# The prompt scores of a differential attention: one fp32 product replaced by two fp32r products over stacked high and low parts

## The chip, the cores and the metric

The kernel runs on one core of a Trainium2 chip. The metric is the device time of one execution in microseconds (us). A profile is one execution taken apart by the hardware profiler; its engines are TensorE (PE, with PEld for its weight loads), VectorE (DVE), ScalarE (ACT), GpSimd (POOL) and SyncE (SP), which here only issues transfers.

## The reference, cut to what matters

One layer of a streaming encoder for 512 prompt tokens and 64 sample tokens, model width 1024, all in float32. A normed input goes through one input projection; its columns feed a gated-delta recurrence (GDN, 4 heads) and a differential attention (4 heads, two components c of 64 columns each for queries and keys, values of 128). Then follow an output projection, an attention over a memory, and a feed-forward stage. The attention that the change is about:

```
s = einsum('bqhcd,bkhcd->bhcqk', qi, kf) * 64 ** -0.5
visible = k_pos[None, :] < ((pi // CHUNK + 1) * CHUNK)[:, None]
s = where(visible, s, -inf)
p = softmax(s, axis=-1)
a = p[:, :, 0] - lam * p[:, :, 1]
return einsum('bhqk,bkhe->bqhe', a, vf)
```

The prompt attends to its own 512 keys in chunks of 64 (causal by chunk); the 64 sample tokens attend to 256 cached keys and their own 64.

## The kernel before, in words

Everything lies transposed, channels in the 128 partitions and tokens in the columns; prompt and sample tokens share one row of T = 576 columns. A weight matrix is loaded in blocks of 128 output columns. `weights` (L165) loads a block, casts it on ACT to its high part in fp32r (`wh`, L161) and subtracts on DVE (`wl`, L162). `project` (L169) multiplies such a block with the high and low parts of the input, in two halves of the tokens: columns 0 to 255 and 256 to 575 (n = 256 and 320). In the first half one multiplication of 512 columns does high weights times both parts of the input, and its two results come out side by side in a bank, to be added by `add_to` (L193: an ACT copy, L194, then a DVE addition, L195); the half has 16 multiplications. The second half has 24 of 320 columns and a single result. The results lie in one of three PSUM banks with the tag `pr`, until a function `evac` has read them.

The program is written in the order of the layer, but the framework orders the instructions of each engine itself: it takes what is ready by its own estimate of the times, earlier code first, and gives each tile a buffer of its tag. On the chip each engine then works through its list in that order, waiting on semaphores. A tile of a tag with one buffer can be written only when the one before has been read for the last time. Work of a later stage is thus found in the gaps of an earlier one. `tc.issue_after` puts instructions behind another one of the same engine.

The stages around the change, in the order of the code:

- GDN. `gdn_prep` (L651) prepares a chunk of 128 tokens for all four heads. Its triangular solve (L734 to L757) goes through levels of two matmul steps, a transpose, and ACT copies (L738 into `Y`, L742 into `X`), the last one L747 to L756, which reads `At` and `Dt`. There are four prompt chunks and a sample chunk; chunks of even number use the tags `At0`, `Dt0`, `Y0`, odd ones `At1`, `Dt1`, `Y1`, with one buffer each (L94). The tags `X`, `KQ` and `vb` have two buffers each for all chunks. `gdn_scan` (L782) then carries the state from chunk to chunk; `gdn_scan_sample` (L817) does the sample's, in pieces between the attention heads. The norms in them take a `pow` on POOL (`rpow`, L207, instruction on L208).
- `diff_project(h)` (L907) projects a head's queries, keys and values. Queries go from PSUM into `qz[h % 2]` (L912 to L919), a tile of two components, where component c has its 64 rows and zeros in the other 64; keys into `kdT` (L920 to L924), which holds all heads; values over a tile `zr` and a transpose into `vtm`. Keys are also transposed into `ko` (L936, which shares the two buffers of `p0`) and stored by SP (L938 to L941).
- `diff_cache` (L947) loads the cached keys and values; its first tile also has the tag `p0` (L948, loads on L951).
- `diff_head(h)` (L957) goes through five query tiles of 128, the sample's first (`t = 4`), then the prompt's four with 128, 256, 384 and 512 keys. For each component a score product goes into bank `g0` or `g1` (L975: the zero rows of `qz` take the other component's keys out of the sum, so `kdT`'s 128 rows serve both); then a maximum (L980), an exponential on ACT (L983), the combination of the two (L987, L988), a zeroing of the padding on POOL for `t = 4` (L990), transposes, and the product with the values. The head's norm, `finish` (L1006), runs in the next head (`between`, L965), with its `pow` on POOL.

The recurrence and the head loop (L1019 to L1026) are followed by the memory's keys and values, the output projection, the memory attention, whose queries are already split into high and low parts (L1160, L1161), and the feed-forward stage.

Of the kernel before, what the change touches and what calls it, by code (L numbers as in the profile page):

```python
# [8 lines left out]
F32 = mybir.dt.float32  # L9
F32R = mybir.dt.float32r  # L10
AF = mybir.ActivationFunctionType
ALU = mybir.AluOpType
# [3 lines left out]
P = 128  # L16
D = 1024
KT = 8
SEQ = 512
DEC = 64  # L20
T = SEQ + DEC
HALVES = ((0, 256), (256, T - 256))
PAST = 256
# [14 lines left out]
def hybrid_layer_kernel(  # L38
# [9 lines left out]
    nc = tc.nc  # L48
    V, A, G = nc.vector, nc.scalar, nc.gpsimd
# [17 lines left out]
    cp = ctx.enter_context(tc.tile_pool(name="cp", bufs=1))  # L67
# [24 lines left out]
    def small(tag, shape, bufs=None, dt=F32):  # L92
        tag = SHARED.get(tag, tag)
        bufs = 1 if tag in ("vn", "on", "S") or tag[:-1] in ("At", "Dt", "Y") else 2  # L94
        return sp.tile(shape, dt, tag=tag, name=nm(tag), bufs=bufs)
# [4 lines left out]
    def bank(tag="ba"):  # L100
        return ps.tile([P, 512], F32, tag=tag, name=nm(tag), bufs=BANKS[tag])
# [4 lines left out]
    def mm(out, lhsT, rhs, start=True, stop=True, pin=False, skip_group_check=False):  # L106
        i = nc.tensor.matmul(out, lhsT, rhs, start=start, stop=stop, skip_group_check=skip_group_check)  # L107
        if pin:
            tc.keep_in_program_order(i)
# [83 lines left out]
    def add_to(dst, b, more):  # L193
        A.copy(dst, more)  # L194
        V.tensor_tensor(dst, b, dst, ALU.add)  # L195
# [244 lines left out]
    for typ in (1, 0, 2):  # L440
# [3 lines left out]
        for h in range(H):  # L444
# [8 lines left out]
            n = SOFF + DEC  # L453
# [21 lines left out]
    with tc.issue_after(behind_keys[1]):  # L475
        ones2, triu2 = const([P, P], "ones2"), const([P, P], "triu2")
        G.memset(ones2, 0.0)
        for i in range(2):
            R = slice(i * DEC, (i + 1) * DEC)
            G.memset(ones2[R, R], 1.0)  # L480
        G.tensor_tensor(triu2, triu, ones2, ALU.mult)
# [8 lines left out]
    V.memset(wab2.bitcast(F32)[:, :, 16:], 0.0)  # L490
    A.copy(wab2[:, :, :8], wab)
    V.tensor_tensor(wab2[:, :, 8:16], wab, wab2.bitcast(F32)[:, :, :8], ALU.subtract)
    abT = small("p0", [16, T + DEC])
    for a0, n in HALVES:
        b = bank("pr")
        for k in range(KT):
# [6 lines left out]
    b = bank()  # L503
# [17 lines left out]
    t1, t2, t3 = gt("t1"), gt("t2"), gt("t3")  # L521
# [19 lines left out]
    def halves_of(dst, src):  # L541

        for i in range(2):
            R = slice(i * DEC, (i + 1) * DEC)
            V.tensor_copy(dst[R], src[R, 4, i::2])

# [24 lines left out]
    for j in range(3):  # L571
        b = bank()
# [321 lines left out]
    od, kdT = e3[:, 0], e5[:, 0]  # L894
# [2 lines left out]
    cv2 = view(e3, 1, 4, 4 * P).rearrange("p (i b) n -> p i b n", i=2)  # L897
    ckT, cvv = cv2[:, 0].rearrange("p b (c n) -> p (b c) n", n=PAST), cv2[:, 1]

    qz = [cp.tile([P, 2, T], F32, tag=f"qz{i}", name=f"qz{i}") for i in range(2)]  # L900
    with tc.issue_after(behind_keys[0]), tc.issue_after(behind_keys[1]):
        for q2 in qz:
            G.memset(q2[64:, 0, :], 0.0)
            G.memset(q2[:64, 1, :], 0.0)
        G.memset(vs[64:], 0.0)

    def diff_project(h):  # L907
        hs = slice(h * P, (h + 1) * P)
        for kind, base in (("q", 2056), ("k", 2568), ("v", 3080)):
            def evac(b, a0, n, more):  # L910
                ts_ = slice(a0, a0 + n)
                if kind == "q":  # L912
                    for c in range(2):
                        R = slice(64 * c, 64 * c + 64)
                        if more is not None:
                            add_to(qz[h % 2][R, c, ts_], b[R], more[R])
                        else:
                            (A.copy if c else V.tensor_copy)(qz[h % 2][R, c, ts_], b[R])
                    return  # L919
                d = small("zr", [P, 320])[:, :n] if kind == "v" else kdT[:, h, ts_]  # L920
                if more is not None:
                    add_to(d, b, more)
                else:
                    V.tensor_copy(d, b)  # L924
                bt = bank()
                for t in range(2):
                    tr(bt[:, t * P : (t + 1) * P], d[:, t * P : (t + 1) * P])
                if a0:
                    tr(bt[:DEC, 256:384], d[:, 256:])
                src, t2 = bt[:, :256].rearrange("p (t d) -> p t d", t=2), slice(a0 // P, a0 // P + 2)  # L930
                if kind == "v":
                    A.copy(vtm[:, t2, hs], src)
                    if a0:
                        A.copy(vs[:DEC, h, :], bt[:DEC, 256:384])
                else:
                    ko = small("ko", [P, 3, P])  # L936
                    A.copy(ko[:, :2], src)
                    nc.sync.dma_start(o_dk_p[0, 0, a0 : a0 + 256, h, :].rearrange("(t p) d -> p t d", p=P), ko[:, :2])  # L938
                    if a0:
                        A.copy(ko[:DEC, 2], bt[:DEC, 256:384])  # L940
                        nc.sync.dma_start(o_dk_s[0, 0, :, h, :], ko[:DEC, 2])  # L941

            project(weights(w2, base + h * P), xs, evac)
        nc.sync.dma_start(o_dv_p[0, 0, :, h, :].rearrange("(t p) d -> p t d", p=P), vtm[:, :, hs])
        nc.sync.dma_start(o_dv_s[0, 0, :, h, :], vs[:DEC, h, :])
# [11 lines left out]
    def diff_head(h, between):  # L957


        hs = slice(h * P, (h + 1) * P)  # L960
        so, co = tiny([P, 5], "ta"), tiny([P, 5], "ta")
        on = small("an", [P, 5, P])
        for t in (4, 0, 1, 2, 3):
            if t == 1:
                between()  # L965
            q0 = QT[t][0]
            nk = q0 + P if t < 4 else PAST + DEC
            nb = (nk + P - 1) // P
            pr = []
            mx, l = tiny([P, 2], "ta"), tiny([P, 2], "ta")  # L970
            for c in range(2):
                b = bank(f"g{c}")
                qq = qz[h % 2][:, c, q0 : q0 + P]
                if t < 4:
                    mm(b[:, :nk], qq, kdT[:, h, :nk])  # L975
                    V.memset(b[:64, nk - 64 : nk], -1e30)
                else:
                    mm(b[:, :PAST], qq, ckT[:, h, :])
                    mm(b[:, PAST:nk], qq, kdT[:, h, SEQ:T])
                V.tensor_reduce(mx[:, c : c + 1], b[:, :nk], AX.X, ALU.max)  # L980
                V.tensor_scalar(mx[:, c : c + 1], mx[:, c : c + 1], -0.125, None, ALU.mult)
                p = small(f"p{c}", [P, 512])
                A.activation(p[:, :nk], b[:, :nk], AF.Exp, bias=mx[:, c : c + 1], scale=0.125, accum_out=l[:, c : c + 1])  # L983
                pr.append(p)
            V.reciprocal(l, l)
            V.tensor_tensor(l[:, 1:2], l[:, 1:2], nlam, ALU.mult)
            V.tensor_scalar(pr[1][:, :nk], pr[1][:, :nk], l[:, 1:2], None, ALU.mult)  # L987
            V.scalar_tensor_tensor(pr[0][:, :nk], pr[0][:, :nk], l[:, 0:1], pr[1][:, :nk], ALU.mult, ALU.add)  # L988
            if nk < nb * P:
                G.memset(pr[0][:, nk : nb * P], 0.0)  # L990
            bt = bank()
            aT = small("aT", [P, 4, P])
            for kb in range(nb):
                tr(bt[:, kb * P : (kb + 1) * P], pr[0][:, kb * P : (kb + 1) * P])
            A.copy(aT[:, :nb, :], v4(bt, nb))
            po = bank("gs")[:, :P]
            for kb in range(nb):
                if t < 4:
                    vv = vtm[:, kb, hs]
                else:  # L1000
                    vv = cvv[:, kb, hs] if kb < 2 else vs[:, h, :]
                mm(po, aT[:, kb, :], vv, start=kb == 0, stop=kb == nb - 1)
            A.activation(pr[1][:, :P], po, AF.Square, accum_out=so[:, t : t + 1])
            A.copy(on[:, t, :], po)

        def finish():  # L1006
            V.tensor_scalar(so, so, 1.0 / P, EPS, ALU.mult, ALU.add)
            rpow(co, so)
            V.tensor_tensor(on, on, co.unsqueeze(2).to_broadcast([P, 5, P]), ALU.mult)
            b, b2 = bank(), bank()  # L1010
            for t in range(4):
                tr(b[:, t * P : (t + 1) * P], on[:, t, :])
            tr(b2[:, :P], on[:, 4, :])
            for src, ts_ in ((b, slice(0, SEQ)), (b2[:, DEC:P], slice(SEQ, T))):
                A.activation(od[:, h, ts_], src, AF.Identity, scale=dn)

        return finish
# [23 lines left out]
    for w, out in ((w_mem_k, o_mk), (w_mem_v, o_mv)):  # L1041
        dst = tokens
        for f in range(2):
            fs = slice(512 * f, 512 * f + 512)
            bs = [bank("pr") for _ in range(2)]
            for kc in range(4):
                wt = split_weights(w[0, 256 * kc : 256 * kc + 256, fs], [P, 2, 512])
                for k in (2 * kc, 2 * kc + 1):
                    for t in range(2):
                        ts_ = slice(t * P, (t + 1) * P)  # L1050
                        for j, (wi, x) in enumerate(((0, mh), (0, ml), (1, mh))):
                            mm(
                                bs[t], x[:, k, ts_], wt[wi][:, k % 2, :],
                                start=(k == 0 and j == 0), stop=(k == KT - 1 and j == 2),
# [6 lines left out]
            if out is o_mk:  # L1061
                for i in range(2):
                    b = bank()
# [79 lines left out]
    for k2 in range(KT // 2):  # L1143
        b = bank()
# [6 lines left out]
    for h in range(H):  # L1151
# [15 lines left out]
        for t, (q0, _) in enumerate(QT):  # L1167
            t0, n = TT[t]
            kk, kl = (mkT, mkl) if t < 4 else (cmT, cml)
            b = bank("gs")  # L1170
            for i in range(2):
                m, q = 2 * h + i, slice(q0, q0 + P)
# [23 lines left out]
        for i in range(2):  # L1196
            b, b2 = bank("g0"), bank("g1")
# [384 lines left out]
```

## Time and profile before

| what | us |
|---|---|
| median of three runs | 1025.71 |
| lowest and highest of them | 1025.43, 1027.94 |
| the profiled execution | 1028.23 |
| its span, from the first to the last instruction | 1026.5 |
| PE busy in the span | 1003.6 |
| DVE busy | 706.8 |
| ACT busy | 537.0 |
| POOL busy | 57.1 |

Times inside a profile are counted from the start of the span. A row of a group of instructions reads: line, engine, operation, output tile <- input tiles, how many, the shortest, median and longest duration in ns, and the start of the first and of the last. Tile names are given without their numbers, so `g` stands for `g0` and `g1`, `At` for `At0` and `At1`; buffers that share a tag are shown under one name (`p` for `p0`, `p1`). A line inside a helper (L107 for matmuls, L113 for transposes) is shared by all its callers. A fp32 matmul appears as two records, one in fp32r as one; the shape column prints f32 for both. Matmuls are pipelined, so their durations overlap, and the distance between the starts of two tells what one costs.

### The profile page before, as it was taken

The numbers are of one execution on the slowest core, as the hardware profiler recorded it, in microseconds if no ns is written. First come the engines' busy times: TensorE is split into PE (matmuls) and PEld (weight loads), VectorE is DVE, ScalarE is ACT, GpSimd is POOL, SyncE is SP. The second block draws the span as 40 slices with busy tenths as digits, with TensorE's granted clock in tenths as the row PEclk, the third lists the DMA queues.
The fourth block names the chain that finished last, engine by engine and source line by source line (L and its number), as shares of the span: only waits on it lengthen the run. The fifth ranks groups of instructions, "written<-read, shape, count | busy, mean of one in ns | idle before, by whom it ended". The sixth has DMA issues, their size and how long they took to land.

```text
span 1026.5 us, 17294 instructions
## 1 busy us (share of the span) xinstructions
PE 1003.6 (98%) x6630; PEld 921.1 (90%) x6630; DVE 706.8 (69%) x1529; ACT 537.0 (52%) x1170; POOL 57.1 (6%) x123
## 2 busy tenths in 40 slices
PE   9999999999999999999999999999999999999996
PEld 7989899998888877899988899999999999999986
DVE  6576785776566676665665787667766677777883
ACT  6654664343465665444444557655544555555434
POOL 3431010100000000000000000000000000000000
PEclk9999999999999999999999999999999999999998
DMA  7332320100312355523211233332222222222202
GB/s 217 122 104 78 107 74 21 44 21 22 104 53 75 100 177 189 172 84 115 62 42 42 62 114 93 114 93 83 83 83 83 83 83 83 82 83 83 82 1 93
DMA packets 121255, 89.99 MB, mean 88 GB/s; under 512 B 5507, under 2 KB 112129, under 8 KB 120661
## 3 DMA queue, kind: packets, MB, share of 16 engines
q1 hardware_dynamic: 120804, 88.24, 28.6%
q8 instruction: 52, 0.85, 0.3%
q10 hardware_dynamic: 368, 0.66, 0.2%
q14 instruction: 31, 0.25, 0.1%
HBM read 79.14 MB, written 9.74 MB: 87 GB/s over the span
## 4 chain that ended last, share of the span: by engine, by line
PE 84%; DVE 4%; issue 3%; ACT 3%; POOL 2%; DMA 1%; POOLq 0%; ACTq 0%; DVEq 0%; SPq 0%
PE pr L107 49%; PE g L107 14%; PE ba L107 10%; PE gs L107 7%; PE ba L113 2%; PE g L113 2%; DVE wl L162 0%; DMA raw<-in_w_ff_dram 0%; POOL tg L208 0%; DVE p L457 0%; DMA out_dram<-S 0%; DMA S<-in_state_gdn_dram 0%; POOL X L604 0%; DMA r<-in_w_ff_dram 0%; DVE on L780 0%
## 5 line engine op out<-in xcount | busy, mean ns | idle before, releaser
L107 PE MATMUL pr<-u,wh 128*128 128x320 f32 (+2 forms) x1240 | 328.2, 342 | 2.1 <-DVE p L323 1.0
L107 PEld LDWEIGHTS pr<-u,wh 128*128 128x128 f32 x1240 | 211.6, 188 | 18.6 <-DVE p L323 1.3
L107 PE MATMUL pr<-u,wl 128*128 128x256 f32 (+1 forms) x816 | 227.7, 303 | 0.0
L107 PEld LDWEIGHTS pr<-u,wl 128*128 128x128 f32 x816 | 149.7, 189 | 3.7 <-issue 0.7
L162 DVE TENSOR_TENSOR wl<-raw,wh 128x1024 fp32r<-128x1024 f32 x65 | 79.5, 1223 | 34.4 <-ACT wh L161 32.5
L107 PE MATMUL pr<-u,w2h 128*128 128x320 f32 (+1 forms) x384 | 99.2, 343 | 2.8 <-DVE u L1415 2.8
L161 ACT CAST wh<-raw 128x1024 fp32r<-128x1024 f32 x65 | 68.2, 1049 | 58.0 <-PE pr L107 52.2
L1330 ACT CAST w2h<-r 128x512 fp32r<-128x512 f32 x56 | 34.7, 620 | 93.6 <-PE pr L107 89.9
L107 PE MATMUL pr<-f,w2h 128*128 128x320 f32 (+1 forms) x288 | 73.8, 340 | 0.0
L107 PEld LDWEIGHTS pr<-u,w2h 128*128 128x128 f32 x384 | 65.9, 191 | 7.9 <-DVE u L1415 3.1
L107 PE MATMUL pr<-u,w2l 128*128 128x256 f32 (+1 forms) x256 | 65.8, 298 | 0.0
L1415 DVE TENSOR_TENSOR u<-u,pr 128x256 f32<-128x256 f32 x96 | 42.9, 449 | 18.5 <-PE pr L107 17.6
L107 PE MATMUL ba<-u,wl 128*128 128x288 f32 x360 | 52.9, 295 | 0.6 <-ACT keep L1366 0.5
L107 PEld LDWEIGHTS pr<-f,w2h 128*128 128x128 f32 x288 | 48.7, 188 | 4.2 <-issue 1.2
L107 PEld LDWEIGHTS ba<-u,wl 128*128 128x128 f32 x360 | 49.2, 188 | 1.2 <-ACT keep L1366 1.2
L107 PEld LDWEIGHTS pr<-u,w2l 128*128 128x128 f32 x256 | 47.5, 191 | 1.5
L107 PE MATMUL pr<-f,w2l 128*128 128x256 f32 (+1 forms) x192 | 48.8, 295 | 0.0
L1331 DVE TENSOR_TENSOR w2l<-r,w2h 128x512 fp32r<-128x512 f32 x56 | 38.5, 688 | 11.3 <-ACT w2h L1330 10.8
L208 POOL TENSOR_TENSOR tiny<-tiny,nhalf 128x1 f32<-128x1 f32 (+4 forms) x10 | 9.2, 924 | 633.7 <-DVE tiny L1479 542.0
L107 PE MATMUL pr<-wh,u 128*128 128x512 f32 x128 | 41.2, 400 | 0.0
L107 PEld LDWEIGHTS pr<-f,w2l 128*128 128x128 f32 x192 | 35.2, 188 | 1.1
L1375 ACT ACTIVATE c<-c 128x288 f32<-128x288 f32 x48 | 20.9, 442 | 28.1 <-DVE c L1374 28.1
(462 smaller groups left out, 2078.5 us busy)
## 6 DMA issues: line engine op xcount, KB each, us to landing
raw<-in_w_ff_dram SPq DMA_DIRECT2D x36, 512.0 KB
raw<-in_w_in_dram SPq DMA_DIRECT2D x28, 512.0 KB
r<-in_w_ff_dram SPq DMA_DIRECT2D x56, 256.0 KB
raw<-in_w_mem_k_dram SPq DMA_DIRECT2D x8, 512.0 KB
raw<-in_w_mem_v_dram SPq DMA_DIRECT2D x8, 512.0 KB
raw<-in_w_out_dram SPq DMA_DIRECT2D x8, 512.0 KB
raw<-in_w_mem_q_dram SPq DMA_DIRECT2D x8, 512.0 KB
raw<-in_w_mem_o_dram SPq DMA_DIRECT2D x8, 512.0 KB
```

What stands on the lines that cost most here:

```text
L107: i = nc.tensor.matmul(out, lhsT, rhs, start=start, stop=stop, skip_group_check=skip_group_check)
L113: i = nc.tensor.transpose(out, in_, ident[:n, :n])
L161: A.copy(wh, raw)
L162: V.tensor_tensor(wl, raw, wh.bitcast(F32), ALU.subtract)
L208: G.tensor_tensor(out, in_, bc(nhalf[: in_.shape[0], 0:1], list(in_.shape)), ALU.pow)
L1330: A.copy(wh, src)
L1331: V.tensor_tensor(wl, src, wh.bitcast(F32), ALU.subtract)
L1375: A.activation(c, c, AF.Relu)
L1415: V.tensor_tensor(am, am, b, ALU.add)
```

## The change

The 32 score products of prompt tiles no longer multiply in fp32. Queries and keys are split into a high part (rounded to fp32r) and the low rest, and three of the four partial products are formed in two fp32r multiplications. For component c, the tile `qs[h % 2]` holds the high parts of the queries in its own 64 rows and the low parts in the other 64 (they took the zeros' place); `ks[c]` holds the high parts of the component's keys in both halves of the rows. Their product over 128 rows is high x high plus low x high. A second product over the component's own 64 rows adds high queries x low keys (`kl`). The sample tile keeps its fp32 products, on a smaller `qz` with the last 128 columns only.

For this the queries' `evac` merges the two results of the first half into `zr`, casts (`hi`) and subtracts (`lo`), and sends each component's 64 rows of both to `qs` by four transfers issued on POOL; the second half is cast and subtracted straight from its bank, and its last 128 columns are also copied into `qz`. Keys get a cast, a subtraction and four POOL transfers for each half of 256 columns. The new tiles use tags of the GDN stage: `hi` and `lo` of the queries `At1` and `Dt1`, `hi` of the keys `Y1`, `ks` `X` and `KQ`, `kl` `vb`; `ks` and `kl` are one tile each for all four heads. `abT`, a small tile before the GDN stage, moves from the tag `p0` to `an`.

```diff
-    abT = small("p0", [16, T + DEC])
+    abT = small("an", [16, T + DEC])
...
-    qz = [cp.tile([P, 2, T], F32, tag=f"qz{i}", name=f"qz{i}") for i in range(2)]
+    qs = [cp.tile([P, 2, T], F32R, tag=f"qz{i}", name=f"qs{i}") for i in range(2)]
+    ks = [small(tag, [P, SEQ], dt=F32R) for tag in ("X", "KQ")]
+    kl = small("vb", [P, SEQ], dt=F32R)
+    own = [slice(64 * c, 64 * c + 64) for c in range(2)]
     with tc.issue_after(behind_keys[0]), tc.issue_after(behind_keys[1]):
+        qz = [small("qlast", [P, 2, P]) for _ in range(2)]
         for q2 in qz:
             G.memset(q2[64:, 0, :], 0.0)
             G.memset(q2[:64, 1, :], 0.0)
...
                 if kind == "q":
+                    if more is not None:
+                        q = small("zr", [P, 320])[:, :n]
+                        add_to(q, b, more)
+                        b = q
+                    hi, lo = (small(tag, [P, 320], dt=F32R)[:, :n] for tag in ("At1", "Dt1"))
+                    A.copy(hi, b)
+                    V.tensor_tensor(lo, b, hi.bitcast(F32), ALU.subtract)
                     for c in range(2):
-                        R = slice(64 * c, 64 * c + 64)
-                        if more is not None:
-                            add_to(qz[h % 2][R, c, ts_], b[R], more[R])
-                        else:
-                            (A.copy if c else V.tensor_copy)(qz[h % 2][R, c, ts_], b[R])
+                        nc.gpsimd.dma_start(qs[h % 2][own[c], c, ts_], hi[own[c]])
+                        nc.gpsimd.dma_start(qs[h % 2][own[1 - c], c, ts_], lo[own[c]])
+                    if a0:
+                        for c in range(2):
+                            (A.copy if c else V.tensor_copy)(qz[h % 2][own[c], c, :], b[own[c], n - P :])
                     return
...
+                if kind == "k":
+                    hi, t2 = small("Y1", [P, 256], dt=F32R), slice(a0, a0 + 256)
+                    A.copy(hi, d[:, :256])
+                    V.tensor_tensor(kl[:, t2], d[:, :256], hi.bitcast(F32), ALU.subtract)
+                    for c in range(2):
+                        for to in own:
+                            nc.gpsimd.dma_start(ks[c][to, t2], hi[own[c]])
...
-                qq = qz[h % 2][:, c, q0 : q0 + P]
                 if t < 4:
-                    mm(b[:, :nk], qq, kdT[:, h, :nk])
+                    mm(b[:, :nk], qs[h % 2][:, c, q0 : q0 + P], ks[c][:, :nk], stop=False)
+                    mm(b[:, :nk], qs[h % 2][own[c], c, q0 : q0 + P], kl[own[c], :nk], start=False)
                     V.memset(b[:64, nk - 64 : nk], -1e30)
                 else:
-                    mm(b[:, :PAST], qq, ckT[:, h, :])
-                    mm(b[:, PAST:nk], qq, kdT[:, h, SEQ:T])
+                    mm(b[:, :PAST], qz[h % 2][:, c, :], ckT[:, h, :])
+                    mm(b[:, PAST:nk], qz[h % 2][:, c, :], kdT[:, h, SEQ:T])
```

## The prediction

> **What bounds the kernel now.** I read the shares of the engines first, then the chain of waits, then the stretches around the edited code.
>
> ```profile
> PE 1003.6 (98%) x6630; PEld 921.1 (90%) x6630; DVE 706.8 (69%) x1529; ACT 537.0 (52%) x1170; POOL 57.1 (6%) x123
> PE 84%; DVE 4%; issue 3%; ACT 3%; POOL 2%; DMA 1%; POOLq 0%; ACTq 0%; DVEq 0%; SPq 0%
> ```
>
> TensorE (PE) is the only engine near its limit and makes 84% of the chain. But a busy share of 98% says that something was always in flight, not that the array was full. So the stage has to be cut up. The columns are the stretch, its length, busy us of PE, PEld, DVE, ACT, POOL, then the clock.
>
> ```profile
> 181.00:257.00 76.00, 74.97 (x594) 68.75 (x593) 54.02 (x126) 28.90 (x53) 6.46 (x6) 1.00 0.11 28
> 257.00:288.00 31.00, 30.29 (x204) 26.72 (x205) 18.03 (x47) 13.01 (x34) 1.01 (x1) 1.00 0.36 103
> 288.00:390.00 102.00, 99.91 (x584) 82.25 (x583) 72.16 (x229) 63.60 (x204) 5.71 (x8) 1.00 0.33 108
> ```
>
> The recurrent (GDN) layers' chunks run to about 270, the differential attention from 279 to 390, both with PE covered. The tile `qz`, which holds a head's queries, shows that the two overlap:
>
> ```profile
> L107 PE MATMUL g<-u,qz x96: 218/379/697, 279.2 to 376.6; 128*128 128x256 f32 x32, 128*128 128x64 f32 x16, 128*128 128x128 f32 x16, 128*128 128x384 f32 x16
> L194 ACT COPY qz<-pr x8: 358/366/368, 147.7 to 327.0; 64x256 f32<-64x256 f32 x8
> L195 DVE TENSOR_TENSOR qz<-pr,qz x8: 398/422/428, 148.7 to 328.5; 64x256 f32<-64x256 f32 x8
> L918 DVE COPY qz<-pr x4: 475/480/483, 156.9 to 335.1; 64x320 f32<-64x320 f32 x4
> L918 ACT COPY qz<-pr x4: 421/421/421, 158.4 to 337.9; 64x320 f32<-64x320 f32 x4
> ```
>
> The scores start at 279, yet head 0's queries leave PSUM at 147.7 and 156.9. The projections of heads 0 and 1 are pulled forward and fill PE while a GDN chunk waits for ACT and DVE. Those reading the projection banks `pr` say how many (window 147 to 290 and stretch 181 to 257):
>
> ```profile
> L924 DVE COPY u<-pr x2: 483/484/485, 194.4 to 266.0; 128x320 f32<-128x320 f32 x2
> L924 DVE COPY zr<-pr x2: 481/482/483, 213.6 to 281.3; 128x320 f32<-128x320 f32 x2
> L195 DVE TENSOR_TENSOR u<-pr,u x2: 425/425/425, 177.8 to 252.0; 128x256 f32<-128x256 f32 x2
> 181.00:257.00 76.00, 27.04 (x123) 18.69 (x123) 3.12 (x7) 1.90 (x5) 1.00 0.11 28
> ```
>
> Keys of head 0 are done at 194.4, values at 213.6, the first half of head 1's keys at 252.0. A half of 256 columns is 16 multiplications and one of 320 is 24; the 123 in the last row are key half 2 of head 0, its values, head 1's queries and its first key half (24 + 40 + 40 + 16 = 120). This filling is what I think the change disturbs.
>
> **The change, part by part.** *Scores.* Each of the 32 prompt score products (4 heads, 2 components, tiles with 128, 256, 384, 512 keys) is fp32 now; the 96 records above, 16 of them 128x512, are two for each product. The chain prices a product of 512 keys, the timeline an fp32r multiplication by its start:
>
> ```profile
> 351.17 0.86 PE g L107 x2
> 281.04 0.40 PE L107 MATMUL pr<-u,wh 128*128 128x512 f32 x1
> 281.27 0.28 PE L107 MATMUL pr<-u,wl 128*128 128x256 f32 x1
> 281.39 0.40 PE L107 MATMUL pr<-u,wh 128*128 128x512 f32 x1
> 200.82 0.44 PE g L113 x4
> ```
>
> 0.86 us for 512 columns is 1.68 ns a column; from 281.04 to 281.39 a 512 and a 256 go by, 0.46 ns a column. One component of a head has 1280 columns: 2.15 us now, 1.18 us in two fp32r passes. A pass of 128 columns I take at 0.11, like the transposes in the last row, and not at 0.06, which adds 0.10. So 2.15 - 1.28 = 0.87, times 8 components: **7.0 us less on PE**. The second pass multiplies 64 rows, which no row shows at fp32r: at worst it costs what one fp32 record does (0.84 ns a column), and 3.9 us are left; at best 128 columns stream at 0.06 and it is 7.8.
>
> *Splitting.* A head's queries lose the copies in the five rows of `qz`: ACT 2 x 0.37 + 0.42, DVE 2 x 0.42 + 0.48. What comes has its like in the memory attention:
>
> ```profile
> L1160 ACT CAST aT<-zr x4: 405/406/408, 474.1 to 521.9; 128x256 fp32r<-128x256 f32 x4
> L1161 DVE TENSOR_TENSOR ql<-zr,aT x4: 415/417/425, 476.0 to 522.7; 128x256 fp32r<-128x256 f32 x4
> ```
>
> Queries: one merge (0.37 ACT, 0.42 DVE), two casts and subtractions (0.41 and 0.42 here, 0.42 and 0.48 at 320), two small copies (estimate 0.26 and 0.2, below the 0.42 and 0.48 of the wide ones). Keys: two casts and two subtractions. In all about +1.1 us ACT and +1.0 DVE a head, 4.5 and 4 for four heads. They lie beside PE work (ACT has 38 us free in 288 to 390, DVE 30), so I cost them at nothing; with no cover they would be the 4.5.
>
> *Transfers.* Every head gets 16 transfers on POOL (8 of queries, 8 of keys, 64 rows each), 64 in all. No row shows a POOL transfer. The nearest are an SP store and the load that waits for it, and POOL's own small instructions:
>
> ```profile
> 179.37 0.38 SPq L938 DMA_DIRECT2D out_dram<-p  x1
> 181.34 0.35 SPq L951 DMA_DIRECT2D p<-in_cache_diff_k_dram  x1
> 196.48 0.38 SPq L938 DMA_DIRECT2D out_dram<-p  x1
> L208 POOL TENSOR_TENSOR tg<-tg,nhalf 128x8 f32<-128x8 f32 x4 | 6.6, 1649 | 43.9 <-DVE tg L686 43.9
> L208 POOL TENSOR_TENSOR tg<-tg,nhalf 128x4 f32<-128x4 f32 x5 | 5.0, 1010 | 92.5 <-DVE tg L776 83.0 <-DVE tg L686 9.5
> ```
>
> So 0.4 to 1.65 us to issue, I take 1.0, the commoner POOL row; and 2.0 us to land (179.37 to 181.34). Four of them: 6 us. Single buffers make them serial: the second half of the queries may overwrite `hi` and `lo` only when four transfers have read them, and head h+1 may write `ks` only after head h's last score. From that score: 6 us to the first key half, 7 more to the second, some 6 for the last two tiles, 19 us against 102/4 = 25 a head. This is hidden. Behind these waits on POOL stand the zeroing in L990, for which a head's first transposes wait, and the `pow` of L208 (norms); on ACT, the next weights' casts. I put 1 us on it, between nothing and 8 (1 us for each of the 8 half-to-half waits).
>
> The Trainium skill, "DMA: Bandwidth & Descriptors", Rules for kernel authors, speaks against this part: transfers to disjoint partition halves are served one after the other, so it advises one of 128 partitions. Its section Anatomy of one DMA gives about 2.0 us plus bytes/436 GB/s, by which 64 KB take an estimated 2.15 us; no run here shows one. Were all 16 serial at that, a head would need 34 us and the transfers would be the bound: the POOL rival below.
>
> *Buffers.* Now a query half leaves PSUM at once into `qz`. Afterwards the second half (320 columns) stays in its `pr` bank until `At1` and `Dt1` are free, and these belong to GDN chunks 1 and 3. Chunk 3 reads them last here:
>
> ```profile
> L107 PE MATMUL g<-Dt,At x32: 218/218/267, 168.4 to 255.4; 64*64 64x64 f32 x32
> ```
>
> Do buffers go round in program order, or to whoever is ready? The SP rows answer: the cache load at 181.34 (tag `p0`, two buffers) waited for head 0's first key store (179.37) to land, though it stands behind the second store (196.48) too, and the store landed as it issued. It took the first store's buffer in turn, and did not use a free one earlier. By that rule `hi` of head 0 comes after chunk 3, at 255.7; its second half leaves its bank after four transfers and a cast, about 262. Three `pr` banks in turn hold q half 1, **q half 2**, k half 1, k half 2; the next, the first value half, needs the blocked one. So from about 181 to 262 nothing fills PE: 96 of those multiplications are late (values 40, head 1's queries 40, keys 16). At 0.46 ns a column 40 are 6.4 us and 16 are 2.8: 15.6 us, and 3.5 more by 266, when the row shows head 1's second key half done: **19 us moved behind the recurrence**. There PE has no room for it.
>
> What comes back: without filling, GDN runs faster. A level of chunk 3 in ACT's copies:
>
> ```profile
> 231.48 0.59 ACT L742 COPY X<-g 128x512 f32<-128x512 f32 x1 [1.90 <-PE g L113]
> 233.37 0.59 ACT L738 COPY Y<-g 128x512 f32<-128x512 f32 x1 [1.30 <-PE g L107]
> 236.70 0.59 ACT L742 COPY X<-g 128x512 f32<-128x512 f32 x1
> 254.34 0.59 ACT L742 COPY X<-g 128x512 f32<-128x512 f32 x1 [2.37 <-PE g L113]
> ```
>
> One level takes 5.2 us (231.48 to 236.70), and four took 22.9 where 20.9 would do: filling costs these levels only 2 us. Against this, `pr` stands on the chain for a quarter of the stretch (the second entry of the row):
>
> ```profile
> by line: PE g L107 41.7%; PE pr L107 23.9%; PE gs L107 14.1%; PE g L113 11.3%; POOL tg L208 1.3%; PE gs L113 1.2%; PE ba L113 1.1%; DVE on L780 0.9%; DVE tg L774 0.9%; ACT on L773 0.8%; ACT X L742 0.8%; ACT Y L738 0.8%; issue 0.8%; DVE tg L
> ```
>
> 23.9% of 76 is 18 us, so 2 to 18 may come back. I take 7, nearer to the levels: 2 for chunk 3, as much for chunk 2, 3 for the preparations and the slack after 257.
>
> The smaller edits cost nothing: `abT` in another tile is read before 130; zeroing `qz` shrinks from 576 columns to 128, on an idle POOL.
>
> *Sum*: -7 + 19 - 7 + 1 = **+6 us**. The profiled execution's span is 1026.5 in a run of 1028.2; it becomes 1034. The median of the three runs is 2.5 below that run, so I forecast 1031.7, say 1032.
>
> **The rivals.** *Faster:* the filling isn't lost, because buffers are given to whoever is ready or because GDN was held up by PE all along (the 23.9%). Then 12 to 19 come back, and the time is 1025.7 - 7 + 0 to 3, so 1018 to 1022. It decides the case when more than 15 of the 19 return. The two-microsecond row speaks against it.
>
> *POOL-bound:* an issue costs 1.65 us as in the wider L208 row. 16 of them are 26.4 a head, more than the 25 of a head; head 0's transfers reach from 256 to 282 and the keys' second half comes after 290, where tiles 2 and 3 want it. With 1.4 us a head and some 4 at the start this adds 10 to the forecast: 1042. POOL's 5.7 of 102 us speak against it.
>
> *Even:* 12 us return, -7 + 19 - 12 + 1 = +1, near 1026.
>
> **How the numbers follow.** Two times within 0.3% (3 us) cannot be told from no change in a measurement of this kernel. Forecast 0.50, POOL-bound 0.10, even 0.16, faster 0.24. Slower is the first two, 0.60. The range is the low end of the faster case to just above POOL-bound: 1018 to 1045.
>
> **What would show it.** Right: head 0's second query half leaves `pr` after 250 and not at 157; `pr` multiplications in 181 to 257 fall from 123 to about 25, and PE's busy time with them; score products of 512 take about 0.46 on the chain. Wrong: L924 of head 0's values still near 214 (rotation is no bound), or GDN ending before 258 (PE was its bound), or POOL's share over 90% in the heads' stretch. A second pass as slow as an fp32 record would leave 4 of the 7 us.

## The result, and the profile after

The changed kernel takes 1038.62 us (median of 4 runs, 1038.10 to 1039.18) beside 1026.14 for the kernel before on the same chip: a ratio of 1.0111, 95% interval 1.0099 to 1.0123, some 11 to 12 us slower. The forecast was 1032. The sign is right; the size is twice the forecast's, and most of the path to it is another one.

The page of the changed kernel: busy time of the engines (with the share of the span and the instructions), the transfers' queue, and the chain by engine. The span is 1036.6 us, 10.1 more than before.

```profile
PE 1010.1 (97%) x6630; PEld 922.6 (89%) x6630; DVE 708.6 (68%) x1541; ACT 540.1 (52%) x1182; POOL 90.4 (9%) x187
q0 software_dynamic: 5120, 4.46, 2.3%
PE 83%; DVE 4%; issue 3%; ACT 3%; POOL 2%; DMA 1%; POOLq 0%; ACTq 0%; DVEq 0%
```

The same three stretches as in the prediction (length, busy us of PE, PEld, DVE, ACT, POOL, granted clock, DMA share, GB/s):

```profile
181.00:257.00 76.00, 74.93 (x593) 68.67 (x593) 53.26 (x124) 28.47 (x53) 6.45 (x6) 1.00 0.10 28
257.00:288.00 31.00, 28.21 (x183) 25.20 (x181) 18.90 (x45) 13.84 (x34) 14.36 (x25) 0.94 0.64 150
288.00:390.00 102.00, 99.64 (x555) 79.28 (x555) 66.86 (x228) 58.71 (x196) 25.75 (x47) 1.00 0.43 120
```

Up to 257 nothing has changed: 593 multiplications where there were 594. Between 257 and 288 there are 183 where there were 204, and between 288 and 390 there are 555 for 584: PE shows as busy nearly all the time, but gets through less. Compared instruction by instruction, the changed kernel stands 0.25 us behind at 264, 5.9 at 274, 6.6 at 315, 10.5 at 350 and 14.3 at 388; some 4 us come back by 404, where the memory's keys and values follow, which had been begun in the meantime (a cast of their weights near 390 stands only 5.7 behind), and about 10 stay to the end.

The `pr` multiplications alone in 181 to 257, and the readers of the value and query banks in the changed kernel (L935 is L924 of the kernel before):

```profile
181.00:257.00 76.00, 27.04 (x123) 18.71 (x123) 2.23 (x5) 1.12 (x3) 1.00 0.10 28
```
```profile
L935 DVE COPY zr<-pr x2: 484/484/484, 213.7 to 282.1; 128x320 f32<-128x320 f32 x2
```
```profile
L923 DVE TENSOR_TENSOR Dt<-pr,At x4: 482/488/492, 261.6 to 351.7; 128x320 fp32r<-128x320 f32 x4
```

Head 0's second query half does stay in its bank to 261.6, as forecast. But the 123 multiplications are all there, and head 0's second value half leaves its bank at 213.7, as before. The filling that I thought lost went through the other two banks.

**Where the first 5.7 us go.** The chain of waits of the changed kernel from 263.94 to 275 (start, us, what the time went to):

```profile
263.94 0.65 PE g L107 x4
...
264.94 0.42 ACT At L922
265.36 0.51 issue
265.86 0.44 POOL qs L925
...
266.38 0.41 POOL qs L925
...
266.88 0.45 POOL qs L926
...
267.40 1.76 POOL tg L208
269.17 3.68 DMA qs<-Dt
...
272.97 0.49 DVE Dt L923
273.46 0.34 DVE Dt L741
...
273.84 0.44 PE g L113 x2
```

Read it from the end. PE's transpose at 273.84 needs L741, a subtraction of the recurrence's sample chunk. L741 stands on DVE behind L923, head 1's second query half, which may overwrite its staging tile `Dt1` only when the transfer of the first half has read it. That transfer was issued late, because the norm's `pow` (L208) stood between it and its neighbours on POOL, and it took 3.68 us to land. One in-order queue hands the delay to the next: POOL, DMA, DVE, PE. Then the clock follows (stretches of 5 us, the columns as above):

```profile
270.00:275.00 5.00, 2.32 (x14) 1.83 (x15) 2.36 (x8) 0.89 (x4) 3.41 (x8) 0.96 0.98 230
275.00:280.00 5.00, 5.00 (x28) 4.96 (x29) 2.42 (x7) 1.69 (x5) 0.42 (x1) 0.70 0.61 148
280.00:285.00 5.00, 5.00 (x33) 4.50 (x32) 4.14 (x8) 3.73 (x9) 0.00 (x0) 1.00 0.72 216
```

PE is busy 2.32 of 5 us, and afterwards the granted clock is 0.96 and 0.70: (0.04 + 0.30) x 5 = 1.7 us more are lost. The DMA share was 0.98 in 270 to 275: the load of a weight block, issued on SP at 268.33, and one of the memory's cached values, issued at 268.75, were under way beside the transfer. That they slowed it is inferred from their standing at the same time.

Such stretches of lower clock are not the change's alone: the profiled execution of the kernel before shows 0.88 and 0.78 between 560 and 570, where the changed one shows 1.00, and near the end both have one (0.68 in 975 to 980; 0.79 in 985 to 990). The 1.7 us are what the clock takes in this place, not a balance over the whole execution, whose mean is 0.994 before and 0.995 now.

**Where the heads lose.** PE and its weight loads around one score product of 512 keys:

```profile
331.33 0.19 PEld L107 LDWEIGHTS g<-X,qs 128*128 128x128 f32 x1
331.48 0.40 PE L107 MATMUL g<-X,qs 128*128 128x512 f32 x1
331.80 0.18 PEld L107 LDWEIGHTS g<-vb,qs 64*128 64x128 f32 x1 [0.29 <-issue]
331.80 0.50 PE L107 MATMUL g<-vb,qs 64*128 64x512 f32 x1
...
332.23 0.20 PEld L113 LDWEIGHTS ba<-ident,p 128*128 128x128 f32 x2 [0.25 <-issue]
332.24 0.44 PE L113 MATMUL ba<-ident,p 128*128 128x128 f32 x2
```

The weights of the 128-row product are loaded at 331.33, ahead of its start at 331.48. Those of the 64-row product are loaded at 331.80, with its start, and the next 128-row weights again only with the next start, at 332.23: on both sides of the 64-row product the load is no longer beside a matmul. From start to start the 64-row passes take 253, 311, 369 and 427 ns at 128, 256, 384 and 512 columns (means of eight each): 0.46 ns a column, as forecast for fp32r, plus 0.20 us. Added up over the trace from start to next start, the prompt's score products now take 19.1 us. The same sum for the kernel before gives 14.6, but that is too low: in some of its fp32 products another multiplication is recorded 28 ns after the second record starts, and most of the product's time then shows as that one's distance (at 351.47 a `pr` multiplication of 256 columns starts so, and the next start is 0.52 us later, where 0.12 is usual). So for a fp32 product the distance between starts does not always tell the cost. By the 0.86 us of the prediction's chain row the products are 17.2 us, and about 19 if that time is counted back to them, so the two passes are at best no gain on PE.

The transfers' issues on POOL, and the time to landing of all into `qs` (ns, and us):

```profile
L925 POOL DMA_DIRECT2D qs<-At x16: 509/517/762, 257.4 to 351.6; - x16
...
DMA to landing us min/median/max: 1.9/2.0/3.7
```

### The profile page after: what moved, and what is told of

It reads as the page before. It is cut to its first block, busy times and chain, and to the rows that moved or that the text cites. A ratio compares the mean times of both kernels' runs of the same rounds, so it can differ in the third digit from the quotient of the medians.

```text
span 1036.6 us, 17480 instructions
## 1 busy us (share of the span) xinstructions
PE 1010.1 (97%) x6630; PEld 922.6 (89%) x6630; DVE 708.6 (68%) x1541; ACT 540.1 (52%) x1182; POOL 90.4 (9%) x187
## 4 chain that ended last, share of the span: by engine, by line
PE 83%; DVE 4%; issue 3%; ACT 3%; POOL 2%; DMA 1%; POOLq 0%; ACTq 0%; DVEq 0%
PE pr L107 49%; PE g L107 14%; PE ba L107 9%; PE gs L107 7%; PE ba L113 2%; PE g L113 2%; DVE wl L162 0%; POOL tg L208 0%; DMA raw<-in_w_ff_dram 0%; DVE p L457 0%; DMA qs<-Dt 0%; ACT c L1394 0%; POOL X L604 0%; DMA r<-in_w_ff_dram 0%; ACT c L1393 0%
## 5 line engine op out<-in xcount | busy, mean ns | idle before, releaser
L107 PEld LDWEIGHTS pr<-u,wh 128*128 128x128 f32 x1240 | 211.9, 188 | 19.1 <-issue 1.7
L208 POOL TENSOR_TENSOR tiny<-tiny,nhalf 128x1 f32<-128x1 f32 (+4 forms) x10 | 8.2, 822 | 629.5 <-DVE tiny L1497 541.7
L1349 DVE TENSOR_TENSOR w2l<-r,w2h 128x512 fp32r<-128x512 f32 x56 | 38.6, 689 | 11.0 <-ACT w2h L1348 10.5
```

What stands on the lines that cost most here:

```text
L208: G.tensor_tensor(out, in_, bc(nhalf[: in_.shape[0], 0:1], list(in_.shape)), ALU.pow)
L1349: V.tensor_tensor(wl, src, wh.bitcast(F32), ALU.subtract)
```

## The experiments

My theory, from these traces: the second pass on 64 rows takes away PE's saving (A1), and transfers stall the queues of DVE and ACT through staging tiles with one buffer (A2). The rivals are that one of the two is all of it, or that the splitting itself costs. Ratios are to the kernel before, with 95% intervals; 0.001 is 1.03 us. They come from several chips, so ratios are compared. The intervals are 1 to 2.5 us to either side, so a difference of two ratios is known to some 1.5 to 3.5 us.

### Full rows alone

```
-mm(b[:, :nk], qs[h % 2][own[c], c, ...], kl[own[c], :nk], start=False)
+mm(b[:, :nk], qs[h % 2][:, c, ...], kl[c][:, :nk], start=False)   # kl[c]: zeros in the other 64 rows
```

> The second pass of each score product multiplies all 128 rows: the keys' low parts lie in two tiles whose other 64 rows are zero. Theory A (the 64-row pass is the loss on PE): in the trace of the changed kernel a 64-row product of 128, 256, 384, 512 columns takes 253, 311, 369, 427 ns from its start to the next start, that is 0.46 ns a column and about 0.20 us more. 32 such passes cost 6.4 us of which the full-row form is free: 1038.6 - 6.4 = 1032, and the next start comes after 0.23 us at 512 columns. Rival B (the fixed part belongs to any second pass of an accumulation, or PE's time was not what bounds the heads): 1037 to 1039, and the 0.20 us stays in the trace.

Measured: 1.0102 (1.0078 to 1.0126), 0.9 us better than the change and within the intervals: rival B by the time, but not by its sign. On PE the theory holds: in this kernel's timeline the loads are ahead of their matmuls again, and 512 columns go by in 0.24 to 0.27 us.

```profile
332.42 0.19 PEld L107 LDWEIGHTS g<-X,qs 128*128 128x128 f32 x1
332.48 0.44 PE L107 MATMUL g<-X,qs 128*128 128x512 f32 x1
332.52 0.19 PEld L107 LDWEIGHTS g<-vb,qs 128*128 128x128 f32 x1
332.75 0.40 PE L107 MATMUL g<-vb,qs 128*128 128x512 f32 x1
332.75 0.64 PEld L107 LDWEIGHTS gs<-u,aT 128*128 128x128 f32 x4
332.99 0.61 PE L107 MATMUL gs<-u,aT 128*128 128x128 f32 x4
```

The score products now add up to 13.0 us, 6 less than in the change, but the time does not fall with them. Its DVE and ACT timelines show where it goes:

```profile
274.48 0.49 DVE L925 TENSOR_TENSOR Dt<-pr,At 128x320 fp32r<-128x320 f32 x1 [3.99 <-DMA qs<-Dt]
```
```profile
369.55 0.40 ACT L940 CAST Y<-u 128x256 fp32r<-128x256 f32 x1 [2.87 <-DMA KQ<-Y]
```

These are the two longest waits for transfers, 4.0 us on DVE and 2.9 on ACT; with three of `hi` (3.2 us on ACT) they come to 10.1 us between 257 and 400, where the change has 3.8. PE runs short of work at both, and each is followed by a lower clock (the column before the last two):

```profile
270.00:275.00 5.00, 1.39 (x9) 1.08 (x9) 0.97 (x4) 0.37 (x1) 2.52 (x5) 0.81 1.04 232
275.00:280.00 5.00, 4.64 (x21) 4.61 (x22) 2.67 (x10) 1.41 (x4) 1.02 (x2) 0.51 0.34 66
...
370.00:375.00 5.00, 2.28 (x10) 2.12 (x10) 3.70 (x8) 2.80 (x8) 2.03 (x4) 0.71 0.36 65
375.00:380.00 5.00, 5.00 (x25) 4.54 (x24) 0.28 (x2) 1.85 (x8) 1.31 (x2) 0.61 0.49 154
```

(0.19 + 0.49 + 0.29 + 0.39) x 5 = 6.8 us, where the change lost 1.7. The single executions bear this out: three took 1039.4 to 1040.5 us at a mean clock of 0.985 to 0.987, and one took 1035.2 at 0.993, which is about the change's clock. So in the one execution where the lower clock stayed away, full rows were some 4 us faster than in the others.

### Buffers of their own for the second query half

```
-hi, lo = (small(tag, [P, 320], dt=F32R)[:, :n] for tag in ("At1", "Dt1"))
+hi, lo = (small(tag, [P, 320], dt=F32R)[:, :n] for tag in (("B1", "B1") if a0 else ("At1", "Dt1")))
```

> The second query half's high and low parts get buffers of their own, so no cast or subtraction waits for the first half's transfers. Theory A (a subtraction that waits 2.64 us at 273 for a transfer stands on VectorE ahead of the recurrence's own work, and PE waits 2.3 us for that): the lag behind the kernel before, 5.7 us between 264 and 274, falls to about 1; 1033. Rival B (what delays the recurrence there is the norm's power on POOL, queued behind the transfers from 266.3 to 267.4): only the 2.6 us of VectorE's wait or less return, the lag after 274 stays over 3; 1036 to 1038.

Measured: 1.0103 (1.0082 to 1.0124), nothing gained that can be told: rival B by its numbers, but not for its reason. DVE's wait is gone, and ACT now waits in its place, for the keys' staging tile `Y1` (ACT's timeline, and its waits from 257 to 400):

```profile
275.01 0.40 ACT L938 CAST Y<-u 128x256 fp32r<-128x256 f32 x1 [2.72 <-DMA KQ<-Y]
275.32 0.36 ACT L738 COPY Y<-g 128x256 f32<-128x256 f32 x1
```
```profile
ACT Y L938 <- DMA KQ<-Y: 7.0, 4, 2.7
```

The recurrence's copy L738 now stands behind the keys' cast, and PE waits 2.4 us for it; the lag at 274 is 4.65. The wait moved to the next tile of the same kind.

### No transfers

```
-for c in range(2):
-    nc.gpsimd.dma_start(qs[h % 2][own[c], c, ts_], hi[own[c]])
...
-            nc.gpsimd.dma_start(ks[c][to, t2], hi[own[c]])
+for z in (*qs, *ks):
+    G.memset(z.bitcast(F32), 0.0)      # once
```

> Leaves out all 64 transfers; the scores read zeros in the stacked tiles, the splitting and the two passes stay. Theory A (transfers cost the 5.7 us at 264 to 274 and the 2 us on POOL at 315, and the 64-row passes the rest): 1030 to 1031, still above the kernel before by 4 to 5. Rival B (the loss is all in the transfers and what waits for them): below the kernel before by the forecast's 7 us, 1019. Rival C (all on PE): 1037 to 1039.

Measured: 1.0077 (1.0060 to 1.0094), 3.5 us less than the change, between theories A and C. That is half of what theory A gave the transfers, and 8 us remain without a single one.

### One fp32 product on the stacked tiles

```
+mm(b[:, :nk], qs[h % 2].bitcast(F32)[:, c, q0 : q0 + P], ks[c].bitcast(F32)[:, :nk])   # for the two passes
```

> Splitting and transfers stay, but each prompt score is one fp32 product of the stacked tiles; it leaves out the keys' low parts. Theory A (two passes with one of 64 rows cost as much as fp32: 2.39 us a head and component by the starts, against 2.15): 8 x 0.24 = 2 us less than the changed kernel, 1036.6. Rival B (the two passes do save the forecast's 7.0 us, and splitting and transfers alone lose 19): 1045.

Measured: 1.0057 (1.0040 to 1.0074), 5.5 us less than the change. Both expectations miss, rival B by its sign: the fp32 product that the change removed is the cheaper one here. By how much PE's rows alone would make it cheaper is not settled, since starts do not price fp32 products well; the 5.5 us are the measured whole.

### The two passes alone, on 128 rows and on 64

The kernel before, with only the multiplications of the change (and one cast of the keys per half):

```
-    mm(b[:, :nk], qq, kdT[:, h, :nk])
+    mm(b[:, :nk], qq, kr[h % 2][:, :nk], stop=False)
+    mm(b[:, :nk], qq, kr[h % 2][:, :nk], start=False)            # on 64 rows: qq[R], kr[h % 2][R, :nk]
```

> The kernel before with only the matmuls changed: each prompt score is two fp32r products of 128 rows, of queries rounded in their old copies and keys rounded by one more ScalarE cast per half (into X and KQ, by head). No low parts, no subtractions, no transfers; it leaves out the low parts of queries and keys. Theory A (PE's time is what the heads wait for): 7.0 us less than before, 1020 beside a before of 1027. Rival B (the heads are a chain through VectorE and ScalarE, and PE's saving only leaves it idle): 1024 to 1027.

> As e5_passes_only, but the second product multiplies the component's own 64 rows, as the change has it. Theory A (the weights of a 64-row product are not loaded beside the matmul before it, nor those after it beside a 64-row product; 0.20 us for each of 32): e5_passes_only + 6.4 us. Rival B (the 0.20 us is filled by other work): the same as e5_passes_only within 1.5 us.

Measured: 0.9942 (0.9928 to 0.9957) on 128 rows, 6.0 us gained; 1.0033 (1.0021 to 1.0045) on 64 rows, 3.4 us lost. So PE's saving is real and arrives in the time, 6.0 of theory A's 7.0, and the row count of the second pass alone turns it by 9.3 us, more than the 6.4 expected. 7.3 of these lie in the score products themselves (12.0 us from start to start on 128 rows, 19.3 on 64): 4.9 in the 64-row passes, and 2.4 in the 128-row passes ahead of them. Where the other 2 lie was not taken apart. Same stretches, first on 128 and then on 64 rows:

```profile
288.00:390.00 102.00, 99.67 (x612) 85.36 (x611) 74.71 (x232) 66.76 (x210) 5.71 (x8) 1.00 0.38 121
```
```profile
288.00:390.00 102.00, 101.35 (x565) 81.01 (x564) 68.23 (x221) 60.78 (x194) 4.54 (x7) 1.00 0.35 111
```

PE is busy longer on 64 rows and gets through 47 multiplications fewer. Its waits for other engines are short in both (3.1 and 2.6 us between 257 and 410), so they are not the difference.

### Two sets, fewer transfers, full rows: the whole computation

```
-    A.copy(hi, b)                                   # staging tile, then two transfers a component
+    hi = qs[h % 2][own[c], c, ts_]
+    A.copy(hi, b[own[c]])                           # straight into its rows; only lo is sent
...
+    A.copy(kh[own[c], t2], d[own[c], :256])         # kh = ks[h % 2][c]
+    nc.gpsimd.dma_start(kh[own[1 - c], t2], kh[own[c], t2])
```

> The whole computation, with what stood in the way taken out: high parts are cast straight into their own rows of the stacked tiles (8 transfers a head in place of 16, no staging tile for keys), the stacked keys and their low parts have a set for even and one for odd heads, the two query halves have a staging tile each, and the second pass has 128 rows. Theory A (the loss was 6.2 us of 64-row passes and some 9 of casts and subtractions that wait for transfers, with ScalarE's and VectorE's queues behind them): the forecast's saving shows, 1022 to 1027. Rival B (the splitting's instructions in the two queues are a cost of their own, as the run without transfers suggests, which still lost 8): 1030 to 1034.

Measured: 0.9992 (0.9982 to 1.0001), no change against the kernel before that can be told, and 12 us better than the change: the upper end of theory A's range, though PE's saving is used up. Between 257 and 400 neither DVE nor ACT waits for a transfer of the stacked tiles. The kernel makes several edits at once; which of them took these waits away was not separated. The longest of PE's waits between 257 and 410:

```profile
PE ba L113 <- DVE p L1011: 2.5, 3, 1.3
PE ba L113 <- DVE an L1032: 1.2, 1, 1.2
PE gs L107 <- DVE on L780: 0.9, 1, 0.9
```

### Three passes without transfers

```
+    mm(b[:, :nk], qh, ks[h % 2][:, :nk], stop=False)
+    mm(b[:, :nk], qh, kl[h % 2][:, :nk], start=False, stop=False)
+    mm(b[:, :nk], ql[h % 2][c][:, q0 : q0 + P], ks[h % 2][:, :nk], start=False)
```

> The whole computation without any transfer: queries' high and low parts lie in tiles with zeros in the other component's rows, as before, and each score is three fp32r products of 128 rows (high x high, high x low, low x high). By PE's rates a component of a head costs 3 x (1280 x 0.459 ns + 0.05) = 1.9 us against 2.15, 2 us less in all. Theory A (transfers and 64-row passes were the loss): 1024 to 1026. Rival B (the splitting's casts and subtractions cost time of their own, 4 to 8 us): 1029 to 1033.

Measured: 1.0023 (1.0012 to 1.0034), 2.4 us slower: rival B, at its low end. With 2 us saved by the rates, splitting costs about 4.

### Two sets, 64 rows

```
+mm(b[:, :nk], qs[h % 2][own[c], c, ...], kl[h % 2][c][own[c], :nk], start=False)
```

> e7_two_sets with the second pass on the component's own 64 rows again. Theory A (the 64-row price is paid whole where nothing waits for transfers; in the run with full rows and the change's buffers it was swallowed by waits for transfers): e7_two_sets + 6.4 to 10 us, 1034 to 1037, with 0.42 us after each 512-column second product. Rival B (what e7_two_sets gained came from the buffers alone, as full rows alone brought about 1 us): within 2 us of e7_two_sets, 1027 to 1029.

Measured: 1.0083 (1.0069 to 1.0098), 9.3 us over the run with full rows. Theory A.

### Transfers on SP, low parts on POOL

`nc.gpsimd.dma_start` becomes `nc.sync.dma_start` in the first, `V.tensor_tensor(kl...)` becomes `G.tensor_tensor` in the second.

> e7_two_sets with its 32 transfers issued on SP in place of POOL. Theory A (POOL's norm powers and the zeroing, behind which PE's work waits, stand behind transfers that wait for casts): 1 to 2 us faster than e7_two_sets, 1025. Rival B (SP's loads of the next weights stand behind the same waits, and the casts of weights come late): 3 to 8 us slower, 1030 to 1035, with idle before the weights' casts.

> e7_two_sets with the subtractions of the keys' low parts (16 of 64 rows) on POOL in place of VectorE. Theory A (VectorE's queue is what is left of the loss: PE waits 2.5 us in e7_two_sets for its combination of the two exponentials, and the full computation stands 5 us above the passes alone): 1 to 3 us faster, 1024 to 1026. Rival B (a POOL subtraction takes some 2 us, and POOL's powers behind it and the transfers come later): 1027 to 1030.

Measured: 0.9992 (0.9984 to 1.0001) on SP, the same as on POOL. Neither theory: in this kernel, where no cast waits for them, it makes no difference which of the two issues them. With the low parts on POOL 1.0033 (1.0020 to 1.0046), 4 us slower, just above rival B's range, though one subtraction takes less than I had put there; that later powers and transfers are the reason was not shown:

```profile
L946 POOL TENSOR_TENSOR B<-u,KQ x4: 717/732/1073, 265.9 to 321.0; 64x256 fp32r<-64x256 f32 x4
```

### Full rows without transfers

The edits of the first and the third experiment together.

> e1_full_rows without its 64 transfers; the stacked tiles hold zeros, so the scores read zeros in place of queries and keys; buffers, casts and subtractions stay as in the change. Theory A (in e1_full_rows waits for transfers swallowed what full rows saved; without transfers the 64-row price comes off the run without transfers): 1036.3 - 6 to 9, 1027 to 1030. Rival B (the single set of staging and stacked tiles holds casts up with or without transfers, or the splitting's instructions are the cost): 1034 to 1037.

Measured: 0.9978 (0.9967 to 0.9988), theory A and better than its range. With the change's staging tiles the four cases are now complete:

| second pass | with transfers | without |
|---|---|---|
| 64 rows | 1.0111 | 1.0077 |
| 128 rows | 1.0102 | 0.9978 |

64 rows cost 10.2 us where nothing waits for transfers, and transfers cost 12.7 us where the rows are full; together they cost 13.6, not 23. With one of the two taken away the other took most of the gain, which is why full rows alone gained nothing that can be told, and why removing the transfers alone gained only 3.5 us. Of the 9.2 us between the two prices of the transfers, known to some 3 us, 5.1 are the lower clock in the places shown (6.8 against 1.7); by the one execution of full rows at a clock of 0.993 the transfers cost about 9 us there and not 12.7. Why transfers met a loaded DMA in just those places in the run with full rows (share 1.04 in 270 to 275, 1.02 in 360 to 365) was not taken apart. That, and what makes up the other 4, stays open.

## Why the prediction was right, and where it was wrong

The measured ladder, each step a difference of two ratios: passes on full rows -6.0, second pass on 64 rows +9.3, casts and subtractions +4.5 (1.0077 - 1.0033), transfers +3.5 (1.0111 - 1.0077). Sum +11.4. The forecast's: scores -7, filling +19, GDN -7, lateness +1, together +6. Slower came true, but by other costs than those forecast, so that the sum came out on the right side was luck.

- **Buffers: this step failed.** "It took the first store's buffer in turn" was carried over from a tag with two buffers to three banks. The trace shows the opposite: with one bank held to 261.6, head 0's second value half still left its own at 213.7, and all 123 multiplications stayed. The sign of what "would show it wrong" was named (L924 near 214) and came true. The 19 us, and with them the 7 that GDN was to give back, were both zero; their difference of 12 only happened to stand where the 17 us of the other three costs were.
- **Scores: the rate was right, the bound was not.** 0.46 ns a column is what the rows show, and full passes gain 6.0 of the 7.0. The worst case that I allowed for 64 rows, a price per column of an fp32 record, has the wrong form: it is 0.20 us per pass whatever its length, and with the passes around them 32 such passes cost 9.3, more than the saving. (That worst case leaves 3.5 us, not 3.9, with the 0.05 us put on each first pass of 128 columns.) The sign named for being right, about 0.46 us for a product of 512 keys, did not come: it took 0.72 on average from start to start in the changed kernel, and 0.50 with only the passes changed, on 128 rows. The trace of before could have told: it has eight blocks of 64-row matmuls in GDN, in fp32, and at each the loads start only with their matmul, going in and coming out.

```profile
254.74 0.31 PE L107 MATMUL pr<-u,wl 128*128 128x320 f32 x1
254.98 0.54 PEld L107 LDWEIGHTS g<-Dt,At 64*64 64x64 f32 x8 [0.19 <-ACT X L742]
254.98 0.68 PE L107 MATMUL g<-Dt,At 64*64 64x64 f32 x8
255.59 0.20 PEld L113 LDWEIGHTS g<-ident,X 128*128 128x128 f32 x2
255.59 0.44 PE L113 MATMUL g<-ident,X 128*128 128x128 f32 x2
```

The 320 columns ahead take 0.24 us to the next start, where 0.15 is usual; the last of the eight 64-row records takes 0.15, where 0.06 is usual: 0.09 us on each side. I bounded the unknown by its columns alone.

- **Splitting: "I cost them at nothing; with no cover they would be the 4.5."** There was no cover: 4.5 on 64 rows, 3.7 on 128 (0.9978 - 0.9942), each known to some 2 us. ACT had 38 us free and DVE 30; that a queue in order is late for what stands behind a cast, whatever its share, is my reading and not shown: PE's waits for other engines between 257 and 410 come to 4.9 us with the splitting on full rows and 3.1 without, and these 1.8 us are not the 3.7.
- **Transfers: landing right, issue half, lateness too small.** 2.0 us to land as forecast; 0.52 us to issue and not 1.0, so POOL is busy 25.75 of 102 us and the POOL-bound rival falls. For the waits I took 1 us between 0 and 8; it was 3.5, and 12.7 with full rows, beyond the 8. I had listed POOL's `pow` and ACT's casts behind the waits, and not the recurrence's own subtraction L741 on DVE, where the largest one fell.
- **The Trainium skill**, "DMA: Bandwidth & Descriptors": Anatomy of one DMA gives an estimated 2.15 us for 64 KB; the trace has a median of 2.0, from 1.9 to 6.2. By Rules for kernel authors transfers of disjoint partition halves are served one after the other; here they were issued some 0.5 us apart and still landed in a median of 2.0 each, so 2 us are not paid in turn.

## What to carry to other kernels

A pass that multiplies fewer rows is not free beside full ones: look in the weight loads' row whether its load starts ahead of its matmul, and pad with zero rows if it doesn't. The kernel at hand may already show such a load elsewhere. A staging tile that a transfer reads hands the transfer's landing time to the engine that writes it next, and to all that is queued there; write into the final place, or give the tile a second buffer, and mend all such tiles at once, since the wait moves to the next. Where two such costs lie side by side, take both away before judging either.

## What the runs showed of the hardware that was not expected

- Weights of a 64-row product were loaded only at its own start, and those of the next 128-row product at the next start; 0.20 us a pass, 9 to 10 us for 32 passes in three pairs of runs (9.3, 9.3, 10.2). The kernel before shows the same around its 64-row fp32 matmuls, 0.09 us on each side.
- After PE had been short of work for a few us, the granted clock fell for some us: in the change 0.70 in 275 to 280, with full rows 0.51 there. In the change it is 0.50 in 275 to 276 and 276 to 277, so the 1.7 us lost, (0.04 + 0.30) x 5, are 3.4 us at half speed. The Trainium skill, "TensorE: Matmul & The Clock Gate", Part 1: The HAM clock gate, has the clock at half or full only, decided over windows of about 3.4 us; the 3.4 us agree. A PE wait of 2.4 us in the run with own buffers was followed by none (the stretches from 270 to 290 show 1.00), so the length of a wait alone does not decide it.
- Transfers of 64 and 80 KB that land in a median of 2.0 us took up to 6.2 in the change, where the DMA share was 1.02 (365 to 371), and up to 8.3 with full rows (0.96 in 360 to 368). The share alone does not tell: others took 3.7 to 3.9 us at 0.69 (315 to 319) and 0.39 (339 to 343).
